# Two attention heads per step, with their score and value products alternating between the halves of TensorE's array

## The chip, the cores and the metric

The kernel runs on one core of one Trainium2 chip. The metric is the device time of one execution in microseconds (us); lower is better. The engines of a core run side by side, each through its own instructions in a fixed order: TensorE (PE in the profile; its weight loads are PEld), VectorE (DVE), ScalarE (ACT), GpSimd (POOL) and SyncE (SP), which here issues the loads.

## The reference

Two layers of an encoder block over 256 tokens of 1024 features. Each layer is a half step of SwiGLU, a mixer with three branches (an S5 state space model, chunked attention, a convolution), and another half step of SwiGLU:

```python
for l in range(DEPTH):
    x = x + 0.5 * swiglu_ffn(rmsnorm(x, ffn1_norm[l]), ffn1_w_up[l], ffn1_w_down[l])
    h = rmsnorm(x, mix_norm[l])
    u_s5, q, k, v, z_conv, gate_logits = jnp.split(h @ w_in[l], SPLIT_POINTS, axis=-1)
    y_s5 = s5_mixer(u_s5, ...) @ w_br_s5[l]
    y_attn = chunked_attention(q, k, v, ...) @ w_br_attn[l]
    y_conv = conv_module(z_conv, ..., w_br_conv[l])
    g_s5, g_attn, g_conv = jnp.split(jax.nn.sigmoid(gate_logits + b_gate[l]), 3, axis=-1)
    x = x + (g_s5 * y_s5 + g_attn * y_attn + g_conv * y_conv) @ w_out[l]
    x = x + 0.5 * swiglu_ffn(rmsnorm(x, ffn2_norm[l]), ffn2_w_up[l], ffn2_w_down[l])
```

The attention has 8 heads of 64 channels. In chunks of 64 tokens each token sees its own chunk and all earlier ones, so of the scores of a head, 256 queries by 256 keys, two blocks are needed: queries 0 to 127 with keys 0 to 127, and queries 128 to 255 with all 256 keys. To the scores a bias is added, a softmax is taken over the keys, and the probabilities are multiplied with the values.

## The kernel before

The residual stream lies in SBUF with features on partitions, as 8 blocks of 128 features by 256 tokens. Weights stream in from HBM in the order of use, in chunks of eight 128x128 tiles (`raw`). ACT rounds each chunk to a high part (`hi`), DVE takes the remainder (`lo`), and a large product is three matmuls in float32r: `hi` with both parts of the other operand, and `lo` with its high part. These are the ordinary matmuls of what follows: the whole 128x128 array, 256 columns, one profile record each. Small products run in float32; a matmul of these has two records.

The program is first recorded in its logical order (`Recorder.add`, L157) and then ordered by a list scheduler (`schedule`, L217) that has a rough cost for each instruction (`price`, L193). Of the instructions of an engine that are ready by its reckoning, it takes the one of the lowest rank, and of these the first recorded. On PE the branches' small products come ahead of the weight stream as soon as they are ready; on the other engines the branches fill in behind it, attention (rank 1) ahead of the convolution (2), S5 (3) and the next layer's S5 tables (4). `flush` (L264) issues the result; since every instruction is issued at L268, all rows of the profile have that line, and the tiles tell them apart. The order is fixed when the program is built: an engine whose next instruction waits does nothing else.

Attention runs while PE computes the gates (24 blocks of `w_in`) from the weight stream. `head(h)` (L862) does one head:

- two score matmuls into a PSUM bank of the ring `at` (two banks). Their operands have 64 channels, so they use 64 of the array's 128 rows: the upper half for an even head, the lower for an odd one. The transposed q and k lie in the tile `AB`, which also holds the bias and the gates; in the profile the scores are `at<-AB`;
- on DVE two reductions that add the bias and find the maximum (`s<-at,AB`), on ACT two exponentials with their sums, on DVE the reciprocal (`sm`), on ACT two scalings (`s<-s,sm`);
- three transposes into another bank of `at` (`at<-ident,s`), copied out by ACT (`pt<-at`);
- three value matmuls (`ax<-pt,vn`) into 64 of a bank's 128 partitions, so with 64 of the array's 128 columns. Two heads share the one bank of the ring `ax`; after the odd head the bank is split into `ath` and `atl` (the tiles `nat` in the profile), the operands of `w_br_attn`.

The convolution's normalisation (`conv_norm`, L803) is recorded after the heads and uses the same ring `ax`: column sums on PE (`ax<-cv,ones`), a reciprocal root on DVE, the spread to all partitions on PE, and on DVE and ACT the last steps in the tile `cv`, which the products with `w_br_conv` read. `s5_states` (L678) does S5 in 8 blocks; after the fourth and the eighth, 16 matmuls in float32 give the outputs (`y<-mc,cc`, `y<-tbl,cc`), each with 32 of the array's columns: four tiles side by side, four products for each. `s5_gelu` (L728) turns them into the operand `gh` of the GLU.

Of the kernel before, what the change touches and what calls it, by code (L numbers as in the profile page):

```python
# [60 lines left out]
            # the last operand block as late as possible  # L61
# [17 lines left out]
NATIVE = ("w_br_conv", "s5_w_glu", "w_br_s5")      # few columns: float32 products, operands not split  # L79
# [15 lines left out]
TMP = dict(ev=4, th=3, sq=2, sa=2, sc=2, mc=4, s=2, pt=1, cv=2, jk=2)  # L95
# [4 lines left out]
#  # L100
# The program is first recorded in its logical order. Each engine runs its instructions in the order
# of issue, so that order is then chosen by a list scheduler with rough costs (they depend on shapes
# alone): the weight stream and what frees PSUM go first, the mixer's branches fill in.


class Op:
    __slots__ = ("eng", "cost", "lat", "rank", "call", "succ", "npred", "ready", "start", "seq")
# [19 lines left out]
class Recorder:  # L127
    def __init__(self, nc):
        self.ops, self.hist, self.rank = [], {}, 0
        self.rings, self.users, self.first = {}, {}, {}  # L130
        self.tensor = Engine(self, nc.tensor, "pe")
        self.vector = Engine(self, nc.vector, "dve")
        self.scalar = Engine(self, nc.scalar, "act")
        self.sync = Engine(self, nc.sync, "sp")
        self.gpsimd = Engine(self, nc.gpsimd, "pool")
# [20 lines left out]

    def add(self, eng, name, fn, args, kw):  # L157
        op = Op()
        op.eng, op.call, op.rank, op.seq = eng, (fn, args, kw), self.rank, len(self.ops)
        if eng == "pe" and op.rank > 0:  # L160
            op.rank = -1
        op.succ, op.npred = [], 0
        outs = _aps([kw.get("out", args[0] if args else None), kw.get("accum_out")])
        ins = _aps(list(args[0 if "out" in kw else 1:]) + [v for k, v in kw.items() if k not in ("out", "accum_out")])
        op.cost, op.lat = self.price(eng, name, outs, ins, kw)
# [21 lines left out]
        for o in preds.values():  # L187
            o.succ.append(op)
            op.npred += 1
        self.ops.append(op)  # L190

    @staticmethod
    def price(eng, name, outs, ins, kw):  # L193
# [23 lines left out]
    def schedule(self):  # L217
# [4 lines left out]
        wait = {e: [] for e in engs}       # (ready time, seq, op)  # L222
        can = {e: [] for e in engs}        # (rank, seq, op)
# [6 lines left out]
        while left:  # L230
# [33 lines left out]
    def flush(self, tc):  # L264
        with tc.manual_schedule():
            for op in self.schedule():
                fn, args, kw = op.call
                fn(*args, **kw)  # L268


# blocks of x that are loaded ahead of a part (chunk, column) of the weights
# [8 lines left out]
class Builder:  # L280
# [15 lines left out]
    # -- small helpers --  # L296
# [4 lines left out]
    # Tiles of one tag take turns in their slots, so work that runs at its own pace has its own tags.  # L301
# [15 lines left out]
    # -- weight stream --  # L317
# [33 lines left out]
    # -- products: out[feature, token] += w.T @ x --  # L351
    def prod(self, out, keys, ops, ks, start, stop):
        nc = self.nc
        for n, k in enumerate(ks):
# [5 lines left out]
            if not isinstance(ops, tuple):  # L360
                # one pass over both parts; the halves of out are added where it leaves PSUM
# [18 lines left out]
    def quad(self, outs, l, name, cs, ops, nk):  # L380
        """Output blocks that share every operand block as it arrives."""
# [4 lines left out]
    def pair(self, outs, l, name, cs, ops, nk):  # L386
        """Two output blocks whose last operand block is used as late as possible."""
# [5 lines left out]
    # -- 1/sqrt on a small tile: bit-level seed and three Newton steps --  # L393
# [12 lines left out]
    def col_rsqrt(self, terms, inv_n, eps=EPS):  # L406
        """terms: [feature, token] tiles whose squares' sums over all features give the variance."""
# [10 lines left out]
    def spread(self, rc, out):  # L418
        """out[:, token] = rc[token] on every partition."""
# [9 lines left out]
    # -- RMSNorm: operands x*g split in two, 1/rms per token --  # L429
# [33 lines left out]
    # -- SwiGLU half step --  # L463
# [58 lines left out]
    # -- S5: decay and rotation tables --  # L522
# [23 lines left out]
    def s5_tables(self, l):  # L546
        """Returns a list of steps: cos/sin(theta*s) for every state and s, decay, and C times coef."""
# [7 lines left out]
        def small_part():  # L555
# [4 lines left out]
            # B, for products of split operands stacked along the contraction: rows (hi, hi, lo)  # L560
# [35 lines left out]
        def angle(j):  # L596
            # fraction of a turn in [-1/2, 1/2]
# [21 lines left out]
        def coefs():  # L619
# [17 lines left out]
            # C times coef, with the signs under which the four products of a state add up  # L637
# [16 lines left out]
    # -- mixer --  # L654
    def mixer(self, l, after):
# [6 lines left out]
        # u  # L662
# [12 lines left out]
        # S5 states, two groups (128 states) at a time  # L675
        y_ps = {}

        def s5_states(j):  # L678
            if j % 4 == 0:
                # channels of one state block on the same partitions, parts (hi, lo, hi) stacked  # L680
# [27 lines left out]
            # the products with sin take the place of this block's tables  # L708
# [4 lines left out]
            if j % 4 == 3:  # L713
# [3 lines left out]
                cc = st["cc"]  # L717
                for n, (w, i) in enumerate(((0, 0), (2, 1), (1, 1), (2, 0))):
                    for q in range(4):
# [3 lines left out]
                                         start=n == 0, stop=n == 3, tile_position=(0, 32 * q))  # L723

# [3 lines left out]
        def s5_gelu(b):  # L728
            # gelu(y) (tanh form), doubled
# [12 lines left out]
        # conv: GLU with both halves of z  # L742
# [13 lines left out]
        # q, k, v with tokens on partitions  # L756
# [23 lines left out]
        # operands of the gates: normalised, in place  # L780
# [5 lines left out]
        # twice the convolution (hp holds twice the GLU): LayerNorm takes that out, with four times EPS  # L786
# [16 lines left out]
        def conv_norm():  # L803
# [17 lines left out]
            for q in range(2):  # L821
                # silu(v), doubled: v*(1 + tanh(v/2))
# [37 lines left out]
        o_ps = {}  # L860

        def head(h):  # L862
            hp2, r0 = h // 2, 64 * (h % 2)
            q, k = qkT["q"], qkT["k"]
            ps = self.bank("at")
            for c, (o, w) in enumerate(((0, 128), (128, 256))):
                nc.tensor.matmul(ps[:, o:o + w], lhsT=q[r0:r0 + 64, hp2, c * P:(c + 1) * P],
# [226 lines left out]
```

## Time and profile before

| what | value |
| --- | --- |
| time, median of 3 runs (lowest to highest) | 1187.76 us (1187.72 to 1188.9) |
| span of the profiled execution, its own time on the page | 1186.6 us |
| PE busy, share of the span | 1177.4 us, 99% |
| DVE busy | 927.2 us, 78% |
| ACT busy | 645.6 us, 54% |
| mean HBM read | 175 GB/s |

The page gives no other time for the profiled execution than its span, from the first to the last instruction. Matmuls are pipelined, so the busy time of PE tells only that something was in flight. How long one matmul holds the array is read from the distance between starts in the timeline.

### The profile page before, as it was taken

What the parts mean: (1) busy time and instruction counts of PE and PEld (TensorE: products, weight loads), DVE (VectorE), ACT (ScalarE), POOL (GpSimd) and SP (SyncE); (2) the same over time, 40 slices, a digit from 0 to 9 for tenths busy, and PEclk for the clock granted to TensorE, in tenths of its full rate; (3) what the DMA queues carried; (4) which work ended last, traced back from release to release, by engine and by line L of the source; (5) the groups of instructions that cost most, each with busy time, mean ns of one, the idle gap of its engine ahead of it and who ended that gap; (6) DMA issues with size and microseconds to landing.
All of it is one profiled execution on the core that took longest, in us unless ns stands there. A gap on an engine that the chain in (4) does not pass through costs nothing.

```text
span 1186.6 us, 21932 instructions
## 1 busy us (share of the span) xinstructions
PE 1177.4 (99%) x8565; PEld 1097.8 (93%) x8565; DVE 927.2 (78%) x1898; ACT 645.6 (54%) x1171; POOL 13.0 (1%) x32
## 2 busy tenths in 40 slices
PE   8999999999999999999999999999999999999998
PEld 7999989898888999998899999898987999999987
DVE  7999876998789998766676666779987888666654
ACT  6546554787643546645544444557875435444442
POOL 0000000000200000000000000000001000000000
PEclk9999999999999999999999999999999999999999
DMA  7655556554334565555555555565533435555552
GB/s 253 212 181 187 195 182 226 195 178 146 101 131 162 178 196 187 187 178 191 182 178 186 187 179 190 184 213 198 192 126 94 152 126 194 194 179 182 189 198 89
DMA packets 59751, 209.97 MB, mean 177 GB/s; under 512 B 6912, under 2 KB 9088, under 8 KB 59392
## 3 DMA queue, kind: packets, MB, share of 16 engines
q1 hardware_dynamic: 58496, 207.79, 50.9%
q8 instruction: 67, 1.10, 0.4%
q0 software_dynamic: 1152, 0.79, 0.3%
q14 instruction: 36, 0.29, 0.1%
HBM read 206.72 MB, written 1.05 MB: 175 GB/s over the span
## 4 chain that ended last, share of the span: by engine, by line
PE 98%; DMA 1%; DVE 0%; ACT 0%; SPq 0%; issue 0%; DVEq 0%
PE mm L268 72%; PE at L268 22%; PE ax L268 2%; PE y L268 1%; DMA px<-in_x 1%; PE pq L268 0%; SPq L268 0%; DVE x L268 0%; DVE acc L268 0%; ACT sq L268 0%; DVE lo L268 0%; DVE ev L268 0%; ACT x L268 0%; DVE px L268 0%; ACT ev L268 0%
## 5 line engine op out<-in xcount | busy, mean ns | idle before, releaser
L268 ACT CAST hi<-raw 128x1024 fp32r<-128x1024 f32 (+1 forms) x373 | 389.8, 1047 | 406.8 <-issue 166.7
L268 DVE TENSOR_TENSOR lo<-raw,hi 128x1024 fp32r<-128x1024 f32 (+1 forms) x373 | 454.9, 1221 | 165.7 <-ACT hi L268 161.9
L268 PE MATMUL mm<-x,hi 128*128 128x256 f32 x2736 | 505.8, 284 | 1.9 <-ACT hi L268 1.8
L268 PEld LDWEIGHTS mm<-x,hi 128*128 128x128 f32 x2736 | 424.5, 189 | 11.4 <-issue 7.4
L268 PE MATMUL mm<-x,lo 128*128 128x256 f32 x1368 | 388.3, 285 | 0.4 <-DVE lo L268 0.2
L268 PEld LDWEIGHTS mm<-x,lo 128*128 128x128 f32 x1368 | 257.2, 188 | 4.7 <-issue 3.8
L268 PE MATMUL mm<-AB,hi 128*128 128x512 f32 x704 | 246.6, 398 | 0.0
L268 PE MATMUL mm<-AB,lo 128*128 128x256 f32 x704 | 193.1, 281 | 0.0
L268 PE MATMUL at<-x,hi 128*128 128x256 f32 x1040 | 188.6, 282 | 0.1
L268 PEld LDWEIGHTS at<-x,hi 128*128 128x128 f32 x1040 | 160.6, 189 | 0.3 <-ACT hi L268 0.3
L268 PEld LDWEIGHTS mm<-AB,hi 128*128 128x128 f32 x704 | 130.6, 188 | 29.7
L268 PE MATMUL at<-x,lo 128*128 128x256 f32 x520 | 146.6, 282 | 0.0
L268 PEld LDWEIGHTS mm<-AB,lo 128*128 128x128 f32 x704 | 132.9, 189 | 2.6
L268 PEld LDWEIGHTS at<-x,lo 128*128 128x128 f32 x520 | 97.9, 188 | 0.0
L268 PE MATMUL mm<-tbl,hi 128*128 128x256 f32 x256 | 46.3, 284 | 0.0
L268 PE MATMUL at<-hi,x 128*128 128x512 f32 x128 | 41.0, 396 | 0.0
L268 PEld LDWEIGHTS mm<-tbl,hi 128*128 128x128 f32 x256 | 39.9, 192 | 0.3 <-ACT tbl L268 0.3
L268 ACT ACTIVATE th<-ev 128x256 f32<-128x256 f32 x88 | 36.2, 412 | 7.2 <-DVE ev L268 7.0
L268 ACT CAST AB<-ev 128x256 fp32r<-128x256 f32 x88 | 34.9, 400 | 6.5 <-DVE ev L268 6.2
L268 DVE SCALAR_TENSOR_TENSOR ev<-th,ev 128x256 f32<-128x256 f32 x88 | 36.8, 419 | 1.2 <-ACT th L268 1.2
L268 DVE TENSOR_TENSOR AB<-ev,AB 128x256 fp32r<-128x256 f32 x88 | 36.6, 419 | 0.4 <-ACT AB L268 0.2
L268 DVE TENSOR_TENSOR ev<-mm,rb 128x256 f32<-128x256 f32 x56 | 23.6, 424 | 15.6 <-PE mm L268 13.5
(222 smaller groups left out, 1174.1 us busy)
## 6 DMA issues: line engine op xcount, KB each, us to landing
raw<-in_w SPq DMA_DIRECT2D x371, 512.0 KB, 3.7
lo<-in_w SPq DMA_DIRECT2D x10, 512.0 KB, 4.4
AB<-in_b SPq DMA_DIRECT2D x2, 1536.0 KB, 7.9
mc<-in_s SPq DMA_DIRECT2D x8, 192.0 KB, 4.1
out_x<-px SPq DMA_DIRECT2D x8, 128.0 KB, 3.2
raw<-in_w SPq DMA_DIRECT2D x2, 256.0 KB, 3.8
px<-in_x SPq DMA_DIRECT2D x1, 512.0 KB, 7.7
ct<-in_p SPq DMA_DIRECT2D x2, 256.0 KB, 3.7
```

The costliest lines, as they stand in the source:

```text
L268: fn(*args, **kw)
```

## The change

A recorded step may now hold several PE instructions: between `together()` and `apart()` all go into one `Op`, with the sum of their costs and the union of what they wait for, and are issued one behind another. `heads(hp2)` replaces `head(h)` and takes an even and an odd head. Their four score matmuls are one such step, alternating between the upper and the lower half of the array, into two `at` banks. Each head's three transposes are a step. The six value matmuls are a step, alternating between the two halves of the columns. The 16 matmuls of S5's outputs are a step too. `pt` has two buffers. The instructions' number, shapes and operands stay as they were.

```diff
-TMP = dict(ev=4, th=3, sq=2, sa=2, sc=2, mc=4, s=2, pt=1, cv=2, jk=2)
+TMP = dict(ev=4, th=3, sq=2, sa=2, sc=2, mc=4, s=2, pt=2, cv=2, jk=2)
...
+    def together(self):
+        self.open = Op()
+        self.open.call = None
+
+    def apart(self):
+        self.open = None
...
+        more = self.open is not None and self.open.call is not None
+        if self.open is not None:
+            assert eng == "pe"
+            op = self.open
+        else:
+            op = Op()
+        if more:
+            op.call.append((fn, args, kw))
...
+        cost, op.lat = self.price(eng, name, outs, ins, kw)
+        op.cost += cost
...
-                fn, args, kw = op.call
-                fn(*args, **kw)
+                for fn, args, kw in op.call:
+                    fn(*args, **kw)
...
+                nc.together()
                 for n, (w, i) in enumerate(((0, 0), (2, 1), (1, 1), (2, 0))):
                     for q in range(4):
...
+                nc.apart()
...
+        def heads(hp2):
...
+            pss = [self.bank("at") for _ in range(2)]
+            nc.together()
+            for c, (o, w) in enumerate(blocks):
+                for e in range(2):
+                    r0 = 64 * e
+                    nc.tensor.matmul(pss[e][:, o:o + w], lhsT=q[r0:r0 + 64, hp2, c * P:(c + 1) * P],
+                                     rhs=k[r0:r0 + 64, hp2, :w], start=True, stop=True, tile_position=(r0, 0))
+            nc.apart()
...
+                pst = self.bank("at")
+                nc.together()
+                for i in range(3):
+                    nc.tensor.transpose(pst[:, i * P:(i + 1) * P], s[:, i * P:(i + 1) * P], self.ident)
+                nc.apart()
...
+            o = self.bank("ax")
+            nc.together()
+            for i, (t, c0, first, last) in enumerate(((0, 0, True, True), (0, P, True, False), (1, P, False, True))):
+                for e in range(2):
+                    r0, h = 64 * e, 2 * hp2 + e
+                    nc.tensor.matmul(o[r0:r0 + 64, c0:c0 + P], lhsT=vn[:, t, h * HD:(h + 1) * HD],
+                                     rhs=pts[e][:, i * P:(i + 1) * P], start=first, stop=last, tile_position=(0, r0))
+            nc.apart()
+            self.split(o[:, :T], ath[:, hp2, :], atl[:, hp2, :])
```

What this does to the order shows at three places. A row is one instruction, or several alike (x2); the numbers are those of the tiles, `mm` is a bank of the weight stream, `hi` and `lo` are its chunks.

PE, first layer, the second head's scores before:

```order
L268 MATMUL mm_755<-x_286_379,hi_749 128x256 x2
L268 MATMUL at_615<-AB_507 128x128
L268 MATMUL at_615<-AB_507 128x256
L268 MATMUL pq_680<-us_675,bs_138 128x256 x2
L268 MATMUL mm_755<-x_286_379,lo_750 128x256
```

PE at the scores of the first two heads now:

```order
L289 MATMUL mm_755<-x_286_379,hi_749 128x256 x2
L289 MATMUL at_608<-AB_507 128x128
L289 MATMUL at_609<-AB_507 128x128
L289 MATMUL at_608<-AB_507 128x256
L289 MATMUL at_609<-AB_507 128x256
L289 MATMUL mm_755<-x_286_379,lo_750 128x256
L289 MATMUL mm_755<-x_286_379,hi_749 128x256 x2
```

The scores of head 0 and head 1, which had a dozen rows of the stream between them, stand together and alternate.

PE, first layer, the value products of head 4 before (`pt_639`), then the transposes of head 5 (`s_642`) and between these the scores of head 7 (`at_654`), and one product of S5's outputs:

```order
L268 MATMUL mm_775<-x_286_379,hi_769 128x256 x2
L268 MATMUL ax_640<-pt_639,vn_506 64x128 x3
L268 MATMUL at_645<-ident,s_642 128x128
L268 MATMUL at_654<-AB_507 128x128
L268 MATMUL at_645<-ident,s_642 128x128 x2
L268 MATMUL at_654<-AB_507 128x256
L268 MATMUL y_692<-mc_687,cc_194 32x256
```

PE now, the last two of the six value products of heads 0 and 1 and what follows:

```order
L289 MATMUL ax_620<-pt_614,vn_506 64x128
L289 MATMUL ax_620<-pt_619,vn_506 64x128
L289 MATMUL at_621<-AB_507 128x128
L289 MATMUL at_622<-AB_507 128x128
L289 MATMUL at_621<-AB_507 128x256
L289 MATMUL at_622<-AB_507 128x256
L289 MATMUL mm_767<-x_286_379,hi_761 128x256 x2
```

The value products of two heads alternate, and the scores of heads 2 and 3 come directly behind them; of the eight value steps six are followed by scores in this way. Transposes no longer stand between the scores of a head, as they did for six of the sixteen, and the products of S5's outputs no longer stand alone: twelve did, three in each of the four blocks of 16.

DVE, first layer, the end of the convolution's normalisation before (`sa` is S5's, `AB<-AB,mm` gates the attention's output):

```order
L268 TENSOR_SCALAR cv_672<-cv_561,px 128x256
L268 SCALAR_TENSOR_TENSOR AB_507<-AB_507,mm_816 128x256
L268 SCALAR_TENSOR_TENSOR cv_561<-cv_671,cv_672 128x256
L268 TENSOR_TENSOR sa_707<-sa_707,sc_708 128x256
L268 TENSOR_SCALAR cv_674<-cv_561,px 128x256
L268 SCALAR_TENSOR_TENSOR AB_507<-AB_507,mm_820 128x256
L268 SCALAR_TENSOR_TENSOR cv_561<-cv_673,cv_674 128x256
```

DVE now, at the same place:

```order
L289 SCALAR_TENSOR_TENSOR sa_1259<-sc_1260,sa_1259 128x256
L289 TENSOR_SCALAR sc_1263<-iota,f_1256 128x256
L289 TENSOR_SCALAR sc_1266<-iota,f_1256 128x256
L289 TENSOR_TENSOR cv_561<-cv_561,cv_667 128x256 x2
L289 SCALAR_TENSOR_TENSOR sa_1262<-sc_1263,sa_1262 128x256
L289 TENSOR_SCALAR cv_672<-cv_561,px 128x256
L289 TENSOR_SCALAR sc_1269<-iota,f_1256 128x256
L289 SCALAR_TENSOR_TENSOR cv_561<-cv_671,cv_672 128x256
L289 TENSOR_SCALAR cv_674<-cv_561,px 128x256
L289 SCALAR_TENSOR_TENSOR cv_561<-cv_673,cv_674 128x256
```

The last steps of `cv` now stand behind S5's scans and between steps of the next layer's tables (`sa`, `sc` of 1259 to 1269). On PE its column sums (`ax_660<-cv_561`) were row 1689 of the order and are now row 1819, behind the last heads' value products (row 1801). The first product with `cv` was row 1895 and is now row 1897, behind four of the GLU's products. PE's first product with the last heads' `nat` now comes four ordinary matmuls behind their value products. In the second layer the order is alike, but no steps of tables stand there. The order of the loads on SP is the same but for two chunks of `w_br_conv` and `s5_w_glu`, which are issued two or three places later; POOL's order is the same.

## Rows read from the trace of the kernel before

**Rows 1.** The page: span, section 1, and shares by engine of section 4.

```profile
span 1186.6 us, 21932 instructions
PE 1177.4 (99%) x8565; PEld 1097.8 (93%) x8565; DVE 927.2 (78%) x1898; ACT 645.6 (54%) x1171; POOL 13.0 (1%) x32
...
PE 98%; DMA 1%; DVE 0%; ACT 0%; SPq 0%; issue 0%; DVEq 0%
```

**Rows 2.** Who PE waited for: engine, line, releaser, us in total, times, longest.

```profile
PE mm L979 <- ACT iota L975: 2.3, 1, 2.3
PE mm L268 <- ACT hi L268: 1.8, 1, 1.8
```

**Rows 3.** Timeline, PE, one head's scores: start us, us, engine, line, operation, out<-in, instructions.

```profile
281.28 0.40 PE L268 MATMUL mm<-x,hi 128*128 128x256 f32 x2
281.52 0.28 PE L268 MATMUL mm<-x,lo 128*128 128x256 f32 x1
281.73 0.92 PE L268 MATMUL at<-AB 64*128 64x128 f32 x4
282.58 0.51 PE L268 MATMUL mm<-x,hi 128*128 128x256 f32 x2
282.92 0.28 PE L268 MATMUL mm<-x,lo 128*128 128x256 f32 x1
```

**Rows 4.** Timeline, PE, one head's value products.

```profile
291.05 0.40 PE L268 MATMUL mm<-x,hi 128*128 128x256 f32 x2
291.38 0.87 PE L268 MATMUL ax<-pt,vn 128*64 128x128 f32 x6
292.18 0.39 PE L268 MATMUL mm<-x,lo 128*128 128x256 f32 x1
292.41 0.40 PE L268 MATMUL mm<-x,hi 128*128 128x256 f32 x2
```

**Rows 5.** Timeline, PE, one product of S5's outputs alone.

```profile
301.91 0.28 PE L268 MATMUL mm<-x,lo 128*128 128x256 f32 x1
302.12 0.62 PE L268 MATMUL y<-mc,cc 128*32 128x256 f32 x2
302.67 0.50 PE L268 MATMUL mm<-x,hi 128*128 128x256 f32 x2
303.00 0.29 PE L268 MATMUL mm<-x,lo 128*128 128x256 f32 x1
```

**Rows 6.** Timeline, PE, around the last 13 products of S5's outputs.

```profile
361.89 0.28 PE L268 MATMUL mm<-nat,hi 128*128 128x256 f32 x1
362.10 0.83 PE L268 MATMUL y<-mc,cc 128*32 128x256 f32 x9
...
363.95 0.39 PE L268 MATMUL mm<-nat,hi 128*128 128x256 f32 x1
364.17 0.28 PE L268 MATMUL mm<-nat,lo 128*128 128x256 f32 x1
```

**Rows 7.** The chain that ended last: start us, us, engine, tile, instructions, same products.

```profile
362.17 1.84 PE y L268 x26
```

**Rows 8.** Stretch, us, busy PE, PEld, DVE, ACT, POOL; clock, DMA share, GB/s.

```profile
281.73:365.73 84.00, 84.00 (x633) 71.15 (x632) 68.37 (x167) 45.59 (x100) 5.96 (x12) 1.00 0.39 131
866.90:951.79 84.89, 84.89 (x636) 71.75 (x636) 69.24 (x168) 46.41 (x102) 5.81 (x12) 1.00 0.36 123
```

**Rows 9.** Who DVE waited for, 280 to 362 us.

```profile
DVE nat L268 <- ACT nat L268: 2.4, 3, 1.1
DVE sm L268 <- ACT s L268: 1.4, 2, 1.0
```

**Rows 10.** Timeline, DVE: the convolution's last step, and a later table step.

```profile
358.47 0.42 DVE L268 SCALAR_TENSOR_TENSOR cv<-cv,cv 128x256 f32<-128x256 f32 x1
...
370.25 0.68 DVE L268 TENSOR_TENSOR bs<-mc,bs 32x512 fp32r<-32x512 f32 x1
```

**Rows 11.** Timeline, ACT: the first head's probabilities.

```profile
285.69 0.81 ACT L268 ACTIVATE s<-s,sm 128x128 f32<-128x128 f32 x2 [0.23 <-DVE sm L268]
```

More of the change, by code (lines that the diff above doesn't have):

```diff
@@ L92 @@
 NPC, NSM = _n, PCOLS["ct"][0]
-TMP = dict(ev=4, th=3, sq=2, sa=2, sc=2, mc=4, s=2, pt=1, cv=2, jk=2)
+TMP = dict(ev=4, th=3, sq=2, sa=2, sc=2, mc=4, s=2, pt=2, cv=2, jk=2)
 BANKS = dict(mm=3, at=2, y=1, pq=1, ax=1)
 class Op:
-    __slots__ = ("eng", "cost", "lat", "rank", "call", "succ", "npred", "ready", "start", "seq")
+    __slots__ = ("eng", "cost", "lat", "rank", "call", "succ", "npred", "preds", "ready", "start", "seq")
 def _aps(vals):
@@ L155, in region @@
         return ap.tensor.name, p0, p0 + dims[0][1], f0, f0 + sum(a * (n - 1) for a, n in dims[1:]) + 1
-    def add(self, eng, name, fn, args, kw):
[L158 to L162, printed above, removed]
+    def together(self):
+        self.open = Op()
+        self.open.call = None
+    def apart(self):
+        self.open = None
+    def add(self, eng, name, fn, args, kw):
+        more = self.open is not None and self.open.call is not None
[6 more added lines that the diff above has]
+            op.call.append((fn, args, kw))
+        else:
+            op.eng, op.call, op.rank, op.seq = eng, [(fn, args, kw)], self.rank, len(self.ops)
+            if eng == "pe" and op.rank > 0:
+                op.rank = -1
+            op.succ, op.npred, op.cost, op.preds = [], 0, 0.0, {}
         outs = _aps([kw.get("out", args[0] if args else None), kw.get("accum_out")])
         ins = _aps(list(args[0 if "out" in kw else 1:]) + [v for k, v in kw.items() if k not in ("out", "accum_out")])
-        op.cost, op.lat = self.price(eng, name, outs, ins, kw)
+        cost, op.lat = self.price(eng, name, outs, ins, kw)
+        op.cost += cost
         preds = {}
@@ L186, in add @@
                 self.users.setdefault(r[0], []).append(op)
[L187 to L190, printed above, removed]
+        for q, o in preds.items():
+            if q not in op.preds and o is not op:
+                op.preds[q] = o
+                o.succ.append(op)
+                op.npred += 1
+        if not more:
+            self.ops.append(op)
     @staticmethod
@@ new lines, in heads @@
+            blocks = ((0, 128), (128, 256))
+            pss = [self.bank("at") for _ in range(2)]
[6 more added lines that the diff above has]
+            nc.apart()
+            pts = []
@@ new lines, in heads @@
+            for e in range(2):
+                h, ps = 2 * hp2 + e, pss[e]
+                s = self.tmp("s", 3 * P)
+                mx, sm = self.small(2, "mx"), self.small(2, "sm")
+                for c, (o, w) in enumerate(blocks):
+                    nc.vector.tensor_tensor_reduce(out=s[:, o:o + w], in0=ps[:, o:o + w],
+                                                   in1=bias[:, h * 384 + o:h * 384 + o + w], scale=1.0,
+                                                   scalar=-3.0e38, op0=ALU.add, op1=ALU.max,
+                                                   accum_out=mx[:, c:c + 1])
+                ts(out=mx, in0=mx, scalar1=-1.0, scalar2=None, op0=ALU.mult)
+                for c, (o, w) in enumerate(blocks):
+                    act(out=s[:, o:o + w], in_=s[:, o:o + w], func=AF.Exp, bias=mx[:, c:c + 1],
+                        accum_out=sm[:, c:c + 1])
+                nc.vector.reciprocal(out=sm, in_=sm)
+                for c, (o, w) in enumerate(blocks):
+                    act(out=s[:, o:o + w], in_=s[:, o:o + w], func=AF.Copy, scale=sm[:, c:c + 1])
+                pst = self.bank("at")
[3 more added lines that the diff above has]
+                nc.apart()
+                pt = self.tmp("pt", 3 * P)
+                act(out=pt, in_=pst[:, :384], func=AF.Copy)
+                pts.append(pt)
@@ new lines, in heads @@
+            o = self.bank("ax")
+            nc.together()
+            for i, (t, c0, first, last) in enumerate(((0, 0, True, True), (0, P, True, False), (1, P, False, True))):
+                for e in range(2):
+                    r0, h = 64 * e, 2 * hp2 + e
+                    nc.tensor.matmul(o[r0:r0 + 64, c0:c0 + P], lhsT=vn[:, t, h * HD:(h + 1) * HD],
+                                     rhs=pts[e][:, i * P:(i + 1) * P], start=first, stop=last, tile_position=(0, r0))
+            nc.apart()
@@ L902, in mixer @@
         self.rank(RANKS[0])
-        for h in range(NH):
-            head(h)
+        for hp2 in range(NH // 2):
+            heads(hp2)
         self.rank(RANKS[1])
```

36 lines of the change are left out of this document (removed).

## Prediction

> **What bounds the kernel now.** I read the page first: PE is busy for 99% of the span, and the chain that ended last is 98% PE [rows 1]. Then the waits of PE: all that the profile knows are about 4 us, nearly all of it at the start [rows 2]. So the time is the sum of what stands in PE's order, and a change pays exactly what it takes out of that order, as long as no wait takes its place. Then the timeline, for what one piece of the order costs. Two ordinary matmuls start at 281.28 and the next at 281.52 [rows 3]: 0.12 us each. Around the small products the distance is longer than their work. The granted clock is 1.00 in both stretches that the change touches [rows 8], the 2.4 GHz level, and I see nothing in the change that would idle PE long enough to move it.
>
> **Price of the small products.** I take the distance between the starts of two ordinary matmuls, one ahead and one behind, less 0.12 for each ordinary one from the first on.
> - Scores of a head: 281.52 to 282.92, three ordinary ones: 1.40 - 0.36 = 1.04 [rows 3].
> - Value products of a head: 291.05 to 292.41, three: 1.36 - 0.36 = 1.00 [rows 4].
> - One product of S5's outputs alone: 301.91 to 303.00, three: 1.09 - 0.36 = 0.73 [rows 5].
> - Thirteen of these together, 26 records [rows 7]: 361.89 to 364.17, two: 2.28 - 0.24 = 2.04 [rows 6].
>
> The last two tell what is inside. The thirteen fall on four column tiles, at most four on one, so eight records follow each other on the fullest tile, where the single product has two. Six further records for 2.04 - 0.73 = 1.31: a record of 256 columns takes 0.22, whether one tile works or four. So column tiles do run side by side, and 0.73 - 2 x 0.22 = 0.3 of the single product is the price of leaving the ordinary form of the array and coming back. By the same measure a head's scores hold the array for 0.65 (two records of 128 columns at 0.11, two of 256 at 0.22) and the switch is 0.39; the six value records hold it for 0.65 and the switch is 0.35.
>
> **What stands in the order before.** Scores: ten heads whole, 10 x 1.04 = 10.4; six parted by transposes, one switch more, 6 x 1.43 = 8.6. Value products: 16 x 1.00 = 16.0. S5's outputs: twelve products alone, 12 x 0.73 = 8.8; the other thirteen of each block, 2.04 twice and, where other work cuts them in three, about 2.3 twice: 8.7. Two of the value steps stand directly at scores, which saves a half switch each, 0.2: -0.4. Sum 52.1 us.
>
> **What stands there now.** Eight steps of scores at 1.04 if both halves work at the same time: 8.3. Eight value steps at 1.00 if both halves work at the same time: 8.0. Four blocks of S5's outputs: 16 products are still eight records on each tile, 4 x 2.04 = 8.2. Six value steps run directly into scores: -1.2. Sum 23.3 us. The gain on PE is 52.1 - 23.3 = 28.8 us, 14.4 in each layer.
>
> The bounds of the two ifs. If the halves took turns, a step would hold the array for another 0.65: 1.69 for scores, 1.65 for values, 5.2 us over eight steps each. For the values I take 1.00 without much doubt, since they use column tiles like S5's outputs. The scores use halves of the rows, and no row here shows two of these together; S5's outputs are the nearest, so I take 1.04 and keep 1.69 as the upper end. Below 1.04 it can't go, because one half alone needs that [rows 3].
>
> On this the Trainium skill (TensorE: Matmul & The Clock Gate, Part 3, "Measured speedup vs the span model") reports 3.07 times for four row tiles, not four. Scaled to two tiles, as an estimate from that page, a step of scores would hold the array 0.20 longer and the sum would be 1.6 us worse; no run here shows it.
>
> At nothing I cost: the transposes, which work in the ordinary form and only stand closer; the second `pt` buffer; and the two later chunk loads on SP, which still land before the GLU as PE has some 48 ordinary matmuls, 5.8 us, between the point that frees their slot and their use. If a load lasted longer than that, PE would wait for the difference.
>
> **What is late next.** DVE. From the first score to the first product with `cv` PE takes 84.0 us in the first layer and 84.9 in the second, and DVE is busy for 68.4 and 69.2 of it [rows 8]. The change takes 14.4 from PE's side and puts four GLU products, 8 x 0.22 = 1.7, ahead of that product: PE now offers 71.3 and 72.2. DVE's side grows: before, its last step on `cv` began at 358.47 [rows 10], 7 us ahead of PE, and now it stands behind S5's last scans, the gelu and, in the first layer, four table steps of 0.68 [rows 10] and eight smaller ones that I put at 0.3 to 0.4. Net of what DVE did in the old stretch after 358.9 I get 4 us more in the first layer, about 72, and nothing more in the second, 69. DVE's waits that hang on ACT and not on PE were 2.4 and 1.4 [rows 9] in the first layer; they remain. So DVE needs 72 + 3.8 = 76 where PE offers 71.3, and 73 where PE offers 72.2: PE waits 4.5 and 1 us. Other DVE waits were for PE itself and shrink as PE comes earlier, but some can stay. As bounds I take 0 (DVE's busy time has tails of neighbouring instructions in it, which would hide this) and 12 (its waits come back in full, and the 0.5 us by which the first product with the last heads' `nat` now comes too soon after their value products grows to a few). I take 5, nearest the two sums.
>
> **The sum.** 1186.6 - 28.8 + 5 = 1162.8 us of span. The median of the runs stands 1.2 above the profiled span (1187.8 - 1186.6), which holds for the new kernel too: **1164 us**.
>
> **Rivals.**
> - *DVE sets the mixer.* If its waits on ACT grow, because two heads' softmax steps now come in one bunch and their reductions queue behind S5's scans, each layer gives back 5 to 8 us rather than 4.5 and 1: 1168 to 1175, say 1171. For it speaks DVE's 68 busy of 84 us, against it that DVE is in order and most of its idle time ended with something PE did late. The Trainium skill has this as a rule (TensorEngine Tiling (Array Packing), "PSUM Bottleneck"): tiling speeds up TensorE but not what empties PSUM. The trace agrees in that DVE was 81% busy there.
> - *The halves of the rows take turns.* PE then pays 5.2 more, and waits less, since DVE gets that time too: 1164 + 5.2 - 2.5 = 1167. Nothing in the trace excludes it.
> - *The change doesn't do what it says:* neither rows nor columns run side by side, and only the saved switches and the joined outputs remain. 10.4 more on PE, no wait left: 1186.6 - 28.8 + 10.4 + 1 + 1.2 = 1170. Rows 6 and 7 speak against it for the columns.
> - *Slower than before:* the chain of a pair becomes the path. Both `at` banks are held by a pair's scores, so the transposes must wait for the softmax, and the next pair can't start. PE in order would wait at the first transposes of each of eight pairs. In the order 54 ordinary matmuls, 6.5 us, stand between the first scores and these transposes. The first head's probabilities were ready at 286.50, 3.9 us after its scores left PE [rows 3, 11], with other steps in between. To eat the 28.8 us, the chain would have to last 6.5 + 3.6 = 10.1 us in all eight, over twice what it took. Unlikely; 1190.
>
> **How the numbers follow.** Forecast (waits of 0 to 8 us, scores side by side) 0.60, with 1159 to 1167; DVE sets the mixer 0.18; rows in turns 0.14; nothing side by side 0.05; slower 0.03. The low end of the range is the sum without any wait, 1186.6 - 28.8 + 1.2 = 1159. The high end takes in the turns of the rows and the larger part of the first rival: 1171. Below 1159 and above 1171 I leave some 0.15. About 0.2%, 2.4 us, is what a measurement of this kernel can tell from no change; every case but the last is far beyond it: faster 0.96, same 0.01, slower 0.03.
>
> **What the next profile would show.** Scores: a row of eight records that lasts 0.9 as the four did, with ordinary starts 1.40 apart around it; 2.05 apart would mean turns. Values: twelve records in about 0.9. S5's outputs: four rows of 32 records, each some 2.0 around. PE's waits: new entries at products with `cv`, `gh` or `nat`, 5 us in all, most in the first layer, with DVE as releaser. DVE's busy share between the first score and `cv`: over 90%. The feed-forward stretches keep their 0.12 per ordinary matmul; if they don't, or if PE's waits exceed 12 us, or if waits appear at the transposes, the reasoning is wrong.

## The result, and the profile after

The changed kernel takes 1166.8 us (median of 4 runs, 1164.65 to 1168.62) where the kernel before takes 1187.7 (1187.4 to 1188.9): the ratio is 0.982, with a 95% interval of 0.9806 to 0.9834. The forecast was 1164 us, with a range of 1159 to 1171. The profiled execution took 1166.6, of which 1164.8 are the span; this answers to 1186.6 in [rows 1].

PE's small products first. In the profile after, L289 is the line that L268 was. The timeline of PE around the first pair's scores, at the last pair's values, at the column sums of the convolution's norm and at the second block of S5's outputs reads (start, us, engine, line, operation, out<-in, tile, form, records):

```profile
281.47 0.39 PE L289 MATMUL mm<-x,hi 128*128 128x256 f32 x2
281.79 0.93 PE L289 MATMUL at<-AB 64*128 64x128 f32 x8
282.65 0.38 PE L289 MATMUL mm<-x,lo 128*128 128x256 f32 x1
282.87 0.40 PE L289 MATMUL mm<-x,hi 128*128 128x256 f32 x2
...
337.49 0.88 PE L289 MATMUL ax<-pt,vn 128*64 128x128 f32 x12
...
340.10 1.02 PE L289 MATMUL ax<-cv,ones 128*128 128x256 f32 x4
...
341.50 1.07 PE L289 MATMUL y<-mc,cc 128*32 128x256 f32 x16
342.38 1.05 PE L289 MATMUL y<-tbl,cc 128*32 128x256 f32 x16
```

Eight score records last 0.93, as four did for 0.92 in [rows 3], and the ordinary starts around them are 1.40 apart, as they were. Twelve value records last 0.88 where six lasted 0.87 [rows 4]. Summed by the same distances, the small products held the array for 52.4 us before and hold it for 23.3 now: 29.1 us less, 14.4 in the first layer and 14.7 in the second.

The span fell by 21.8 only. What came back is read from PE's waits (engine, tile, releaser, us in total, times, longest) and from the timeline where the largest stands:

```profile
PE mm L289 <- DVE cv L289: 4.0, 2, 3.5
PE mm L1011 <- ACT iota L1007: 2.3, 1, 2.3
PE mm L289 <- ACT hi L289: 1.3, 2, 0.8
```

```profile
351.31 1.46 PE L289 MATMUL mm<-gh,lo 128*128 128x256 f32 x6
352.60 0.59 PE L289 MATMUL ax<-sq,ones 128*128 128x256 f32 x2
353.03 0.59 PE L289 MATMUL mm<-gh,lo 128*128 128x256 f32 x2
357.11 0.70 PE L289 MATMUL mm<-cv,lo 128*128 128x256 f32 x2 [3.48 <-DVE cv L289]
...
358.07 1.84 PE L289 MATMUL mm<-cv,lo 128*128 128x256 f32 x4
...
931.61 0.70 PE L289 MATMUL mm<-cv,lo 128*128 128x256 f32 x2 [0.56 <-DVE cv L289]
...
932.58 1.03 PE L289 MATMUL mm<-cv,lo 128*128 128x256 f32 x4
```

The second and the third row of the waits answer to the two of [rows 2], and the first is the one that the change brought. (A wait of 0.6 us for `AB` near 27 us is new too, but the waits of the first 30 us sum to the same: the first scores start at 281.79 where they started at 281.73.) From the start of the last `gh` record to the first `cv` record PE stands 3.86 us in the first layer and 0.94 in the second, 3.64 and 0.72 beyond the 0.22 of a record. Behind the long gap four `cv` records take 1.84 where the second layer's take 1.03. The stretches say why (us, PE busy, granted clock, DMA share, GB/s):

```profile
353.40:357.10 3.70, 0.23 (x2) 1.00 0.23 89
357.10:361.30 4.20, 4.19 (x12) 0.62 0.00 0
```

PE did nothing for 3.6 us at the 2.4 GHz level, and then the granted clock lay at 1.2 GHz for most of 4.2 us. The first 24 starts from the first `cv` product on take 6.97 us in the first layer and 5.29 in the second: 1.7 us. The kernel before shows 1.00 in every stretch of 5 us. So the span goes 1186.6 - 29.1 + 3.6 + 0.7 + 1.7 = 1163.5, and 1.3 us are left that no single row carries.

### The profile page after: what moved, and what is told of

Read it like the earlier page. It is cut to its first block, busy times and chain, and to the rows that moved or that the text cites. A ratio compares the mean times of both kernels' runs of the same rounds, so it can differ in the third digit from the quotient of the medians.

```text
span 1164.8 us, 21936 instructions
## 1 busy us (share of the span) xinstructions
PE 1151.6 (99%) x8565; PEld 1086.8 (93%) x8565; DVE 924.8 (79%) x1898; ACT 643.9 (55%) x1171; POOL 13.0 (1%) x32
## 4 chain that ended last, share of the span: by engine, by line
PE 97%; DVE 1%; DMA 1%; ACT 1%; issue 0%; SPq 0%; ACTq 0%; DVEq 0%
PE mm L289 73%; PE at L289 21%; PE ax L289 1%; DMA raw<-in_w 1%; PE y L289 1%; PE pq L289 0%; DVE cv L289 0%; ACT hi L289 0%; DVE ev L289 0%; DVE lo L289 0%; ACT sq L289 0%; ACT x L289 0%; DVE bs L289 0%; SPq L289 0%; DVE sc L289 0%
## 5 line engine op out<-in xcount | busy, mean ns | idle before, releaser
L289 ACT CAST hi<-raw 128x1024 fp32r<-128x1024 f32 (+1 forms) x373 | 390.0, 1047 | 397.4 <-PE mm L289 189.3
L289 DVE TENSOR_TENSOR lo<-raw,hi 128x1024 fp32r<-128x1024 f32 (+1 forms) x373 | 454.7, 1221 | 157.1 <-ACT hi L289 153.9
L289 PE MATMUL mm<-x,hi 128*128 128x256 f32 x2736 | 502.0, 283 | 1.4 <-ACT hi L289 1.3
L289 PEld LDWEIGHTS mm<-x,hi 128*128 128x128 f32 x2736 | 423.8, 189 | 5.8 <-ACT hi L289 2.7
L289 PE MATMUL mm<-x,lo 128*128 128x256 f32 x1368 | 386.8, 284 | 0.3 <-DVE lo L289 0.2
L289 PEld LDWEIGHTS mm<-x,lo 128*128 128x128 f32 x1368 | 257.0, 188 | 1.9 <-DVE lo L289 0.7
L289 PE MATMUL mm<-AB,hi 128*128 128x512 f32 x704 | 246.6, 398 | 0.0
L289 PE MATMUL mm<-AB,lo 128*128 128x256 f32 x704 | 193.1, 281 | 0.0
L289 PE MATMUL at<-x,hi 128*128 128x256 f32 x1040 | 188.6, 282 | 0.6 <-ACT AB L289 0.6
L289 PEld LDWEIGHTS at<-x,hi 128*128 128x128 f32 x1040 | 160.6, 189 | 0.8 <-ACT AB L289 0.8
L289 PEld LDWEIGHTS mm<-AB,hi 128*128 128x128 f32 x704 | 130.6, 188 | 29.7
L289 PE MATMUL at<-x,lo 128*128 128x256 f32 x520 | 146.5, 282 | 0.0
L289 PEld LDWEIGHTS mm<-AB,lo 128*128 128x128 f32 x704 | 132.9, 189 | 2.6
L289 PEld LDWEIGHTS at<-x,lo 128*128 128x128 f32 x520 | 97.8, 188 | 0.0
L289 PE MATMUL mm<-tbl,hi 128*128 128x256 f32 x256 | 46.5, 284 | 0.0
L289 PE MATMUL at<-hi,x 128*128 128x512 f32 x128 | 41.0, 396 | 0.0
L289 PEld LDWEIGHTS mm<-tbl,hi 128*128 128x128 f32 x256 | 40.1, 192 | 0.1
L289 ACT ACTIVATE th<-ev 128x256 f32<-128x256 f32 x88 | 36.2, 412 | 7.0 <-DVE ev L289 6.9
L289 ACT CAST AB<-ev 128x256 fp32r<-128x256 f32 x88 | 35.0, 400 | 6.7 <-DVE ev L289 6.4
L289 DVE SCALAR_TENSOR_TENSOR ev<-th,ev 128x256 f32<-128x256 f32 x88 | 36.8, 419 | 1.2 <-ACT th L289 1.2
L289 DVE TENSOR_TENSOR AB<-ev,AB 128x256 fp32r<-128x256 f32 x88 | 36.6, 419 | 0.8 <-ACT AB L289 0.7
L289 DVE TENSOR_TENSOR ev<-mm,rb 128x256 f32<-128x256 f32 x56 | 23.6, 423 | 15.8 <-PE mm L289 12.9
```

## Experiments

Each time stands beside the kernel before on the same chip, 1188.2 to 1188.5 us; the changed kernel is at 1166.8.

**One half of the change each.** First S5's outputs alone as one step, with the function for one head of the kernel before:

```
-        for hp2 in range(NH // 2):
-            heads(hp2)
+        for h in range(NH):
+            head(h)
```

> Only S5's output products become one step; the heads stay one by one as before. If the joined outputs are worth what the prediction put down (12 x 0.73 + 8.7 singles-and-pairs less 4 x 2.04 = 9.3 us), and PE still reaches the first product with cv after DVE (it came 7 us late before, and now some 4.6 per layer earlier), nothing is given back: 1187.7 - 9.3 = 1178.4, with no wait for cv. If DVE sets the mixer whatever PE does, part comes back as a wait for cv or gh: 1181 or more.

Measured: 1177.3 us (1176.7 to 1177.9), ratio 0.991. PE waits nowhere for `cv`, and the small products hold the array for 41.4 us, 11.0 less than before. All of that reached the time. The price of 9.3 was 1.7 too low. In this run's trace transposes part the scores of three heads where they parted those of six, since the heads' steps fall elsewhere in the order; at 0.39 a switch that is 1.2 us of the 1.7.

Then the heads alone, with S5's outputs placed one by one:

```
-                nc.together()
                 for n, (w, i) in enumerate(((0, 0), (2, 1), (1, 1), (2, 0))):
...
-                nc.apart()
```

> Only the heads go two at a time; S5's outputs are again placed one by one. Gross gain 28.8 - 9.3 = 19.5, so 1168.2 if no wait appears. The side-by-side theory expects a wait for cv well under the 3.6 us of the full change in the first layer, since PE comes some 4.6 us later there, and 1168 to 1170. That is only some 2 us above the full change: the last 9 us of gross gain would be worth little, because DVE's chain to cv ends no earlier. If instead the waits have nothing to do with how early PE comes, they stay (3.6 and 0.7, and the stretch at the lower granted clock): 1174 to 1175.

Measured: 1175.6 us (1174.7 to 1177.1), ratio 0.990. The gross gain is 19.6, as expected, but 7 us of it came back: the side-by-side expectation of 1168 to 1170 failed and the other one, that the waits stay, held. PE in the first layer:

```profile
344.79 1.02 PE L289 MATMUL ax<-cv,ones 128*128 128x256 f32 x4
...
356.75 1.03 PE L289 MATMUL mm<-gh,lo 128*128 128x256 f32 x4
358.18 0.67 PE L289 MATMUL ax<-sq,ones 128*128 128x256 f32 x2 [0.40 <-DVE sq L289]
362.11 1.22 PE L289 MATMUL mm<-cv,lo 128*128 128x256 f32 x2 [3.26 <-DVE cv L289]
...
363.98 1.91 PE L289 MATMUL mm<-cv,lo 128*128 128x256 f32 x4
```

The stretch behind the wait (us, busy PE, PEld, DVE, ACT, POOL, granted clock, DMA share, GB/s):

```profile
362.10:368.00 5.90, 5.89 (x16) 4.80 (x17) 2.47 (x7) 0.86 (x2) 0.00 (x0) 0.58 0.00 0
```

PE comes to `cv` 5 us later than in the full change (362.11 against 357.11), yet it waits nearly as long (3.26 against 3.48). So the wait is not a due time that DVE misses: the chain that makes `cv` starts from PE's own products (the column sums, then `ax<-sq,ones`), and moves with them. The column sums come 4.7 us later too (344.79 against 340.10), and from them to the first `cv` record it is 17.3 us here and 17.0 in the full change. Behind the wait the clock is 0.58 for 5.9 us, and four `cv` records take 1.91.

**The order inside a step.**

```
-            for c, (o, w) in enumerate(blocks):
-                for e in range(2):
+            for e in range(2):
+                for c, (o, w) in enumerate(blocks):
...
-            for i, (t, c0, first, last) in enumerate(...):
-                for e in range(2):
+            for e in range(2):
+                for i, (t, c0, first, last) in enumerate(...):
```

> The full change, but within a step one head's products all stand before the other's, for scores and for values. If the halves of the array run side by side because neighbouring products fall on different halves, this takes it away: a step of scores should last some 1.7 instead of 1.04 and a step of values some 1.6 instead of 1.0, 8 x (0.65 + 0.6) = 10 us more on PE over both layers, of which the wait for cv swallows some 4 to 6: 1170 to 1173. If the gain came from fewer entries into and exits from tiles alone, the steps last as long as they do in the full change and the time stays at 1166.8.

Measured: 1168.6 us (1168.35 to 1170.7), ratio 0.984. A first pair's scores and a last pair's values in PE's timeline:

```profile
282.76 0.93 PE L289 MATMUL at<-AB 64*128 64x128 f32 x8
...
339.31 1.14 PE L289 MATMUL ax<-pt,vn 128*64 128x128 f32 x12
```

Both expectations missed. The scores last 0.93 in either order. The values take 1.14 for 0.88, 0.26 more per step; by the distances around all steps PE lost 2.2 us, not 10. In the trace's records both heads' 128-column score products start at 282.757 and 282.770, and both 256-column ones at 283.082 and 283.095, though head by head was the order of issue: the halves of the rows ran on their own, whichever came first. For the halves of the columns the order counts a little. So the alternation itself is worth some 2 us of the change, and standing in one step the rest of what the heads gained. This rests on the distances: the times differ by 1.8 us at the median, but also in the granted clock (in the one profiled it lay at 0.53 over 360 to 365 us) and at the start (the first scores come 1.0 us later than in the changed kernel's profile).

**Every product of a step twice,** to see what a further record costs once PE is in the tiles:

```
-            for c, (o, w) in enumerate(blocks):
+            for c, (o, w) in enumerate(blocks * 2):
+                c %= 2
```

and in the same way for the values and for S5's outputs.

> Every product of a step stands in it twice, the second round over the first; the outputs are the same. It measures what 8 more records of scores, 12 more of values and 32 more of S5's outputs cost once PE is in the tiles, without entry and exit. Ordinary float32 products take 0.22 per 256 columns. Side by side: scores 0.33, values 0.33, S5's outputs 0.88 more per step. In turns: 0.66, 0.66 and 3.5. The head-by-head run, where the scores lasted as long in either order, left open which.

The expectation took a product for one record; a float32 product of 256 columns is two records of 0.22 [rows 5], as the prediction had it. Measured: 1178.8 us, in a single execution. With the expectation put right, side by side means 0.65 more for scores and for values and 1.75 for S5's outputs, and turns mean twice and four times as much. PE's timeline:

```profile
282.58 1.58 PE L289 MATMUL at<-AB 64*128 64x128 f32 x16
...
336.31 1.53 PE L289 MATMUL ax<-pt,vn 128*64 128x128 f32 x24
...
342.30 1.07 PE L289 MATMUL y<-mc,cc 128*32 128x256 f32 x16
343.18 1.05 PE L289 MATMUL y<-tbl,cc 128*32 128x256 f32 x16
344.05 1.04 PE L289 MATMUL y<-mc,cc 128*32 128x256 f32 x16
```

Eight more score records cost 1.58 - 0.93 = 0.65, twelve more value records 1.53 - 0.88 = 0.65; sixteen of S5's start 0.87 to 0.88 after the sixteen before them, which is four records of 0.22 on each of four tiles. Two halves of the rows, two halves of the columns and four tiles of the columns run fully side by side. A single head's 1.04 is then 0.65 of work and 0.39 for leaving the ordinary form and coming back. So the gain has two parts: entries saved (eight on scores, eight on values, and those of the parted scores and the single outputs of S5), and the second head's work, 16 x 0.65 = 10.4 us, done beside the first's. The steps grew by 17.4 us in all and the span by 12.2, because the wait for `cv` fell to 0.2 and the clock stayed at its full level: in this order PE has 20 us of other products between the start of the column sums and `cv`, against 13 in the changed kernel.

On this the Trainium skill (TensorE: Matmul & The Clock Gate, Part 3, "Measured speedup vs the span model") models a pack as one product's time and about 4 ns per further tile. These rows bear it out within a few ns for two row tiles: the second half starts 7 ns after the first in the records of the changed kernel (281.794 and 281.801), and the 0.20 per step that the prediction scaled from the page's 3.07 times for four tiles did not show.

**What makes PE wait for cv: the late start or the table steps?** DVE's timeline in the changed kernel, between the last `gh` and `cv`:

```profile
349.80 0.68 DVE L289 TENSOR_TENSOR bs<-mc,bs 32x512 fp32r<-32x512 f32 x1
...
351.84 0.48 DVE L289 TENSOR_SCALAR sq<-ident,y 128x128 f32<-128x128 f32 x2
352.35 1.28 DVE L289 TENSOR_TENSOR bs<-mc,bs 32x512 fp32r<-32x512 f32 x2
353.65 0.35 DVE L289 TENSOR_SCALAR sc<-iota,f 128x256 f32<-128x256 f32 x1
...
354.18 0.42 DVE L289 SCALAR_TENSOR_TENSOR sa<-sc,sa 128x256 f32<-128x256 f32 x1
354.52 0.61 DVE L289 TENSOR_SCALAR sc<-iota,f 128x256 f32<-128x256 f32 x2
355.04 0.76 DVE L289 TENSOR_TENSOR cv<-cv,cv 128x256 f32<-128x256 f32 x2
```

The rows of `bs`, `sa`, `sc` from `iota` are the second layer's S5 tables, which need nothing from the mixer and fill DVE wherever the schedule finds a hole. In the second layer none stand there. The other suspect is that the convolution's norm begins late: its column sums come at 340.10, though its input, the convolution's taps, was done at 281 (322 in the expectation is wrong), because it takes the one bank `ax` behind the last pair of heads. One run moves the norm ahead of that pair:

```
-        for hp2 in range(NH // 2):
+        for hp2 in range(NH // 2 - 1):
             heads(hp2)
         self.rank(RANKS[1])
         conv_taps(0, CW)
         conv_norm()
+        self.rank(RANKS[0])
+        heads(NH // 2 - 1)
```

> The full change, with the convolution's norm recorded ahead of the last pair of heads, so that it takes the one bank ax before that pair does and not after it. If PE waits for cv because the norm stands in that bank's line behind the last heads (its column sums came at 340.1, although the taps were done at 322), then the wait for cv goes in both layers (3.6 and 0.7), and with it the 1.8 us that the lower granted clock after it cost: 1166.8 - 6 = 1161, range 1160 to 1162. If DVE's amount of work is what PE waits for (72.0 busy of 75.3 in the first layer), the wait only moves, to gh or to the last heads' nat, and the time stays within 1.5 us of 1166.8.

Measured: 1170.3 us (1169.8 to 1171.7), ratio 0.985: slower than the changed kernel, which neither theory said. The wait for `cv` is gone in both layers, but others came:

```profile
PE y L289 <- DVE mc L289: 2.8, 2, 1.8
...
PE mm L289 <- DVE nat L289: 1.7, 2, 0.9
...
PE ax L289 <- ACT cv L289: 1.0, 2, 0.5
PE mm L289 <- ACT nat L289: 1.0, 2, 0.5
...
PE mm L289 <- DVE AB L289: 0.4, 1, 0.4
```

Now the last pair stands behind the norm for the same bank (its values start at 345.45, not 337.49), and S5's last outputs behind DVE. The run doesn't tell the two suspects apart, since it put a new line in place of the old. The next three go further. First, the table steps are put behind the first layer's gated sums, by order alone:

```
+        if self.floor is not None:
+            preds[self.floor.seq] = self.floor
...
+                nc.floor = self.last if fill and l else None
                 for f in fill:
                     f()
+                nc.floor = None
...
+        self.last = nc.ops[-1]
         m2 = self.tile(self.big, [P, 2, KD, T], F32R, "tbl")
```

> The full change, with the second layer's S5 table steps ordered behind the first layer's gated sums. They are pure order: nothing waits more or less by semaphores. If the first layer's 3.6 us at cv comes of DVE's table steps (four of 0.68 and some twenty small ones stand between the last heads and cv there, and none in the second layer, where the wait is 0.7), that wait falls to the second layer's 0.7 and the 1.8 us at the lower granted clock go: 1166.8 - 2.9 - 1.8 = 1162. If it is the late start of the convolution's norm that sets the wait, it stays: 1166.8.

Measured: 1161.9 us (1161.45 to 1163.3), ratio 0.978, as the table steps' theory said. PE in the first layer:

```profile
351.77 1.67 PE L291 MATMUL mm<-gh,lo 128*128 128x256 f32 x7
354.01 0.70 PE L291 MATMUL mm<-cv,lo 128*128 128x256 f32 x2 [0.56 <-DVE cv L291]
...
354.98 1.03 PE L291 MATMUL mm<-cv,lo 128*128 128x256 f32 x4
```

The first layer's gap is now the second's, 0.94, and four `cv` records take 1.03 again: the clock stayed at its full level. 2.9 us of wait and 1.7 of clock make 4.6 of the 4.9 gained.

Then the late start, without a new line: the last pair's values take a bank of the ring `at`.

```
-            o = self.bank("ax")
+            o = self.bank("at" if hp2 == NH // 2 - 1 else "ax")
```

> The full change, but the last pair's values go to a bank of the ring at (which its own transposes free) and not to ax, so that the norm may start when the taps are done and the last pair is not put behind it. If the late start alone makes PE wait: no wait at cv in either layer, 1166.8 - 4.3 - 1.8 = 1160.7. If DVE has too much to do ahead of cv, gh and the last nat, which the norm-ahead-of-the-heads run speaks for (there the wait at cv went and others came, 1170.3), the first layer keeps some 3 to 4 us of waits elsewhere and the second about 1: 1165 to 1168.

Measured: 1163.3 us (1163.2 to 1164.2), ratio 0.979, between the two expectations. There is no wait for `cv` at all; instead PE stands once in each layer for a bank that DVE empties late (`AB`), 0.7 to 0.8 us:

```profile
PE mm L289 <- DVE AB L289: 1.5, 2, 0.7
```

DVE's timeline shows that this run changed more than the start:

```profile
352.13 0.68 DVE L289 TENSOR_TENSOR bs<-mc,bs 32x512 fp32r<-32x512 f32 x1
352.85 0.43 DVE L289 SCALAR_TENSOR_TENSOR cv<-cv,cv 128x256 f32<-128x256 f32 x1
...
354.30 0.68 DVE L289 TENSOR_TENSOR bs<-mc,bs 32x512 fp32r<-32x512 f32 x1
```

The column sums now come at 326.1, but only one of the four `bs` steps and none from `iota` stands ahead of the last step on `cv`; the schedule put the others behind it. So either edit takes the long wait away, and either takes the table steps out of the chain. Begun late, the chain ends nearly in time without them; whether one begun early would end in time with them in it, no run shows. Both edits at once:

> Both edits of the two runs before this: the norm starts early and the second layer's table steps come later. If both causes count, no wait is left and the clock stays at its full level: 1160.5, the sum 1186.6 - 29.1 + 1.5 around the span + at most 1.5 of small waits. If the table steps alone count, the same 1162 as with them alone; if neither, 1166.8.

Measured: 1162.7 us (1161.4 to 1163.1), ratio 0.978. The two do not add up; the wait for `AB` stays at 1.5 us, and it is no better than the table steps alone.

**Making the wait on purpose.** In the kernel with the later table steps, second layer only:

```
+            for i in range(12 * l):
+                ts(out=cv[:, i % 2, :], in0=cv[:, i % 2, :], scalar1=1.0, scalar2=None, op0=ALU.mult)
```

> The kernel with the later table steps, with twelve DVE multiplications of cv by 1.0 put into the second layer's chain behind its scaling by the norm, the outputs being the same. They start 0.2 to 0.3 us apart, 2.4 to 3.6 in all, about what the table steps had put ahead of cv in the first layer. If DVE's time ahead of cv passes to PE one for one, the second layer's gap at cv grows from 0.94 to 3.3 to 4.5. If a gap of that length is what makes the granted clock fall, some 1.7 us at the lower clock follow it there, as they did in the first layer of the full change: 1161.9 + 2.4 to 3.6 + 1.7 = 1166 to 1167.2. If the fall belongs to the first layer or to the table steps, the clock stays full: 1164.3 to 1165.5.

Measured: 1166.7 us (1164.1 to 1167.8), ratio 0.982. The twelve steps in DVE's timeline:

```profile
925.61 2.51 DVE L291 TENSOR_SCALAR cv<-cv 128x256 f32<-128x256 f32 x12
```

PE's timeline around the wait:

```profile
924.27 1.89 PE L291 MATMUL mm<-gh,lo 128*128 128x256 f32 x8
929.12 0.70 PE L291 MATMUL mm<-cv,lo 128*128 128x256 f32 x2 [2.96 <-DVE cv L291]
```

The stretches of the wait and behind it (busy PE, PEld, DVE, ACT, POOL, granted clock):

```profile
925.78:929.12 3.34, 0.38 (x2) 0.00 (x0) 3.10 (x15) 0.62 (x2) 0.00 (x0) 1.00 0.28 109
929.12:933.40 4.28, 4.28 (x20) 3.67 (x21) 3.02 (x9) 0.85 (x2) 0.00 (x0) 1.00 0.01 2
```

The 2.4 us of DVE work (2.51 busy) made the gap 2.4 longer, from 0.94 to 3.34: DVE's time ahead of `cv` passes to PE one for one. The clock did not fall in the profiled execution, which is the fastest of the four, 1164.1 at a mean clock of 1.000; the other three took 1166.2 to 1167.8 at 0.997 to 0.998, where all four of the kernel without the twelve steps stayed at 0.999 to 1.000. Where in those three it fell, no trace shows. The changed kernel shows the same: 1164.65 at 0.999, and 1166.6 to 1168.6 at 0.996 to 0.998. So with a gap of this length in the kernel the clock falls in some executions and not in others.

**A version that goes further.** With the later table steps, all of S5's gated products ahead of the convolution's:

```
-GLU = 4
+GLU = 0
```

> The kernel with the later table steps, and S5's gated products all ahead of the convolution's projections (before: four of these first; the stream of weights follows). Eight more records of 0.217, 1.7 us, then stand between the last heads' products and cv, of which PE waits 0.72 beyond its pitch in each layer. If that wait is only a matter of what stands ahead of cv, it goes in both layers: 1161.9 - 1.4 = 1160.5. If gh is as late as cv, a wait for gh takes its place: 1162.

Measured: 1161.45 us (1160.55 to 1162.0), ratio 0.9776 (0.976 to 0.979). No wait for `cv` or `gh` is left, and the profiled span is 1158.8 against 1160.3; the medians differ by 0.4, which the runs can't separate from nothing. Both versions with the later table steps beat the changed kernel by some 5 us, with intervals that don't meet (0.9806 to 0.9834 there).

## Why the prediction was right, point by point

- **What bounds the kernel.** PE's order, and all that leaves it counts unless a wait takes its place. Held: 29.1 left, 4.4 came back as waits and 1.7 at the lower clock. The feed-forward stretches kept their pace, 0.14 us from record to record between 450 and 850 us in both kernels.
- **The price of the small products.** 52.1 before was 52.4 in the sum of the distances, and 23.3 now was 23.3. The upper end kept for the scores, 1.69 per step, did not come; 1.04 did. The rival of turns (1167) is out by the doubled products, and the estimate from the skill's 3.07, 0.20 per step, is out with it.
- **The size of the waits.** 4.5 and 1 were 3.64 and 0.72, at the place and with the releaser that were named. The windows that answer to [rows 8] (busy PE, PEld, DVE, ACT, POOL) show DVE at 96% and 93%:

```profile
281.79:357.10 75.31, 71.84 (x635) 66.17 (x634) 72.03 (x182) 46.79 (x106) 5.97 (x12) 1.00 0.50 156
859.28:931.60 72.32, 71.77 (x635) 66.20 (x634) 67.54 (x167) 44.69 (x102) 5.82 (x12) 1.00 0.47 152
```

- **The reason for the waits was half right.** The prediction got them as a balance: DVE's busy time and its waits against what PE offers. DVE's 72.0 in the first row is the forecast 72. But with the heads alone PE offered 5 us more, which by the balance leaves no wait, and the wait stayed. What counts is the chain from the norm's column sums to `cv`, and the table steps that the forecast did count (four of 0.68 and the smaller ones) count because they stand in that chain: without them 2.9 of 3.64 go. That the balance gave a good number was luck: the same steps stood in both.
- **The step that failed.** "I see nothing in the change that would idle PE long enough to move it", said of the clock, beside a forecast of a 4.5 us wait in one place. Behind the wait the clock fell to 0.62 over 4.2 us, and 1.7 us of the profiled execution were lost to it. With the table steps ordered behind, the long wait and the fall were both gone from the profile.
- **The sum.** Against the 1164 forecast: 0.3 more gain and 0.6 less wait, 1.7 for the clock, 0.6 more around the span (1166.6 - 1164.8 = 1.8 where 1.2 was taken over), 1.3 unassigned: 2.7, and the runs' median is 2.8 above. The 1.2 was mis-sized: it set the median of several executions against the span of one, and every execution that has both on record stands 1.7 to 1.8 above its own span. The one execution of the changed kernel with a mean clock of 0.999 took 1164.65, which puts most of the miss on the clock.
- **DVE sets the mixer.** In the form that was put (5 to 8 us in each layer, by the softmax in bunches) it did not come: DVE's waits for `nat` and `sm` [rows 9] are 0.3 or gone. The rival *slower*, by the chain at the transposes, did not come either: PE waits at none of them.

## What to carry to other kernels

A short excursion into tiles costs its entry and exit first: joining excursions pays more than the order in them, and the order matters where column halves are shared. When products leave the bounding engine, look at the chains that begin at that engine's own products; they keep their length when that engine comes sooner, and filler work that a scheduler put in the hole is now in the way, so order it behind. A wait of a few us on TensorE can cost its clock too (1.7 us behind 3.6 here): price both.

## What the runs showed of the hardware that I had not expected

- Products on the two halves of the rows ran side by side even when all of one half's were issued first (0.93 us for eight records in either order); on halves of the columns, head by head cost 0.26 us more for twelve records (1.14 against 0.88).
- After a gap of 3.3 to 3.9 us on PE the granted clock lay at 1.2 GHz for part of the next 4 to 6 us (0.62, 0.58) in some executions, and stayed at 2.4 GHz in others; after the single gaps of 0.94 it stayed there. With the norm ahead of the last pair it was 0.83 over 920 to 930, where PE's single gaps were under 1.5 us, so a single long gap is not the only thing ahead of a fall. Why it fell in one execution and not in the next, no run here tells.
